# Delta-rule part of a two-layer decoder trunk on one core: TensorE's program order kept and rewritten, own products in one stretch each, inverse by levels

## The chip, the cores and the metric

The kernel runs on one core of one Trainium2 chip. The metric is the device time of one execution in microseconds (us). A core has five engines, each with an instruction stream of its own: TensorE (PE, matrix products into PSUM), VectorE (DVE), ScalarE (ACT), GpSimd (POOL) and SyncE (SP, here the issuer of most DMAs). They wait for each other through semaphores. Times of day below ("at 325.3") are microseconds from the start of the profiled span.

## The reference

`x` is 256 tokens of 1024 channels, float32. Two layers, each a half-step SwiGLU block, a mixer, and another half-step SwiGLU block, with an RMS norm ahead of each:

```
for l in range(DEPTH):                                   # DEPTH = 2
    h = h + 0.5 * swiglu(rms_norm(h, ffn1_norm[l]), ffn1_w_in[l], ffn1_w_out[l])
    u = rms_norm(h, mix_norm[l])
    (z_s, xbc, dt_s, qkv, z_d, b_d, a_d, gate_s, gate_d) = jnp.split(u @ w_in[l], split_points, axis=-1)
    y_s = mamba2_branch(...)                             # SSD, chunks of 128 tokens, 32 heads of 64
    y_d = deltanet_branch(...)                           # gated delta rule, chunks of 64 tokens, 8 heads of 128
    merged = sigmoid(gate_s) * (y_s @ ssm_w_branch[l]) + sigmoid(gate_d) * (y_d @ dn_w_branch[l])
    h = h + merged @ w_out[l]
    h = h + 0.5 * swiglu(rms_norm(h, ffn2_norm[l]), ffn2_w_in[l], ffn2_w_out[l])
return rms_norm(h, final_norm)
```

The change lies in the delta-rule branch. q, k and v pass a causal convolution of four taps and a SiLU. Then, for each head and chunk of 64 tokens:

```
M = where(strict, (kb @ k.T) * decay, 0)                 # kb = k * beta
sol = triangular_solve(eye + M, concat([v * beta, kb * exp(G)]))
u, w = sol[..., :dv], sol[..., dv:]
a_qk = (q @ k.T) * decay
# over the 4 chunks, one after the other:
v_new = u_c - w_c @ state
o = q_c @ state + a_c @ v_new
state = state * exp(gl) + k_c.T @ v_new
```

## The kernel before

**Products and weights.** Every float32 product is made of three products of reduced-precision parts: high·high, high·low, low·high. A weight tile (`wraw`, 128x1024, 512 KB) is fetched by SP into one of 5 buffers; ScalarE copies its high part (`whi`, in `act`, L68); VectorE subtracts to get the low part (`wlo`, in `tt`, L71); 5 pairs of `whi`/`wlo` can wait for TensorE. So each weight tile costs SP, ScalarE and VectorE one instruction each, in the order in which TensorE will use it.

**Bulk units.** The mixer's input projection is cut into units. A unit of channels (`kk`, `qq`, `vv` for k, q, v; `zd` the delta branch's gate; `bc` and `xs` of the SSD branch) takes two weight tiles and 48 products of 128x256 (`chan_chunk`; in the profile its three kinds of product are L340, L345 and L346). A unit of tokens (`t`, for z and the gates) takes two weight tiles and 24 products of 128x512 (L366). Behind each `kk`, `qq`, `vv`, `bc` and `xs` unit stands a convolution (`conv`): for each half an ACT instruction `ca`, three multiply-adds on VectorE (`stt`, L74) and an ACT SiLU that gives `kP`, `qP`, `vP`, a tile with the channels in partitions.

**The delta rule's small work.** Heads go in four pairs, `hp` 0 to 3.
- `turned` (L776): four TensorE transposes of `kP` or `qP` for the norms and for `kd`.
- `own` (L788): the products k·k (`kkb`) and q·k (`qkb`) of a chunk with itself, two heads beside each other. From `kkb` VectorE makes `Q`, the strict triangle M of each head and chunk (`tt`); from `qkb` it makes `AT`.
- `invert`: (I+M)⁻¹ for the 32 blocks of 64x64. The 16x16 diagonal blocks of `Q` go through DRAM (`dq1`, L866) into a layout `X` (L872), where VectorE sweeps over them (15 pairs of `tp` and `X`, then a COPY, L881), and come back (`dq2`, L882; then sixteen small DMAs into `T` and `TT`, L885 and L886). Then two doublings, to 32 and to 64: `yb` = Q·TT (L891), an eviction to `Y`, `wb` = T·Y, an eviction into `TT`. Before, each doubling is done for one half of the blocks after the other.
- `vtb` (L853): transposes of `vP`.
- `recur`: four chunks one after the other: `ksb`, `qsb` (k and q against the state, L954), `rh` on VectorE, `vnb` (L973), `sb` (the state's update, L981, with eight `stt` on VectorE), `ob` (L995).

After this part comes the SSD branch (`cbb`, L1045; `xsb`, L1101 on).

**The order.** The list `ORDER` names the steps in which the program is written: lower-case letters are units, K, Q and V the rest of a unit (turn, own products, norm), I a step of the inverse, R a step of the recurrence. A scheduler then lays out each engine's stream from its estimates and from priorities. The weight tiles follow the order of the units.

Of the kernel before, what the change touches and what calls it, by code (L numbers as in the profile page):

```python
# [16 lines left out]
P = 128  # L17
# [29 lines left out]
z20 s z10 z11 s z21 s M k1 k0 q1 k2 k3 K1 K0 q3 q0 K3 K2 v0 q2 I Q0 I Q3 I z30 v1 z31 Q2 v2 V0 I v3  # L47
V1 I V3 I Q1 V2 d0 R R R b3 R b2 b0 R b1 R d2 R x00 R d1 x01 R d3 R R P R g100 g101 D0 S0 x10 T0 D1
x11 g110 g111 S1 x20 T1 o x21 N D2 y S2 D3 x30 x31 T2 g000 g010 g001 S3 g011 T3
""".split()  # L50


@with_exitstack
def trunk_kernel(ctx, tc, x, wst, wsm, norms, lpar, rpar, cst, out):
    nc = tc.nc
    V, A, G, PE = nc.vector, nc.scalar, nc.gpsimd, nc.tensor
# [191 lines left out]
    for y in Y:  # L248
        G.memset(y[:], 0.0)
# [98 lines left out]
    def tok_chunk(ps, ks):  # L348

# [6 lines left out]
        for t, k0, (wh, wl) in order:  # L356
# [8 lines left out]
            for j, (st, mv) in enumerate(three):  # L365
# [8 lines left out]
                i += 1  # L374

    def chan_chunk(ps, cut=False):

        ws = [take(), take()]
        for a in range(2):
            for q in range(2):  # L380
                wh, wl = ws[q]
                for k in range(4):
                    kt = 4 * q + k
                    c0 = k * 256 + a * P
                    mm3w(
                        ps[:, a * 256 : (a + 1) * 256],
                        wh[:, c0 : c0 + P],
                        wl[:, c0 : c0 + P],
                        uTh[:, kt, :],
                        uTl[:, kt, :],  # L390
                        kt == 0,
                        kt == KT - 1,
                        cut and a == 0 and kt == 1,
                    )

# [197 lines left out]
    def mixer(l, nxt):  # L593
# [17 lines left out]
        def tok_unit(key, part, done):  # L611
# [3 lines left out]
            tok_chunk(open_[key], range(KT) if part is None else range(4 * part, 4 * part + 4))  # L615
# [4 lines left out]
        def z_unit(g, part):  # L620
            if part != 1:
                yz[g] = slots.tile([P, 2, 512], F32, tag=f"y{g}", name="yz")
            tok_unit(("z", g), part, lambda t, ps: act(yz[g][:, t, :], ps[:], AF.Silu))
# [13 lines left out]
        z_unit(0, None)  # L637
# [146 lines left out]
        def own(bank, x, y, hp):  # L784

            for c in range(4):
                for a in range(2):
                    PE.matmul(  # L788
                        bank[64 * a : 64 * a + 64, c * 64 : (c + 1) * 64], x[:, hp, c, a, :], y[:, hp, c, a, :],
                        start=True, stop=True,  # L790
                    )

        qev = {}

        def k_unit(hp):
            ps = accb("kk")
            chan_chunk(ps, hp == 1)
# [3 lines left out]
            def rest():  # L801
                ktb, nb = turned(kP, hp)
                ts(kq[:, hp], nb[:], EPS, ALU.add)
                c1 = small([P, 4], "c1")
                V.reciprocal(out=c1[:], in_=kq[:, hp])
                tt(c1[:], c1[:], Bp[:, hp], ALU.mult)
                stt(c3n[:, hp], c1[:], -1.0, eG[:, hp], ALU.mult, ALU.mult)
                kkb = trb("kkb")
                own(kkb, kP, kP, hp)
                kk = s2.tile([P, 4, 64], F32, tag="s2", name="kk")  # L810
                for c in range(4):
                    act(kk[:, c], kkb[:, c * 64 : (c + 1) * 64], scale=c1[:, c : c + 1])
                for a in range(2):
                    rows_ = slice(64 * a, 64 * a + 64)
                    qev["ins"] = tt(Q[rows_, 4 * hp : 4 * hp + 4, rows_], dN[rows_, 4 * hp : 4 * hp + 4], kk[rows_], ALU.mult)
                for c in range(3):
                    act(kd[:, c, hp, :], ktb[:, c * P : (c + 1) * P], scale=dT[:, 4 * hp + c, 63:64])
                rsqrt(c2[:, hp], kq[:, hp], [P, 4])
                G.tensor_tensor(out=c2[:, hp], in0=c2[:, hp], in1=Bp[:, hp], op=ALU.mult)
                yield  # L820

            return rest()

        def q_unit(hp):
            ps = accb("qq")
            chan_chunk(ps)
# [3 lines left out]
            def rest():  # L830
                _, nb = turned(qP, hp)
                ts(oe[:, hp], nb[:], EPS, ALU.add, EPS * 128.0, ALU.mult)
                qkb = trb("qkb")
                own(qkb, kP, qP, hp)
                for a in range(2):
                    rows_ = slice(64 * a, 64 * a + 64)
                    qk = qkb[rows_, 0:256].rearrange("p (c i) -> p c i", c=4)
                    tt(AT[rows_, 4 * hp : 4 * hp + 4, rows_], dT[rows_, 4 * hp : 4 * hp + 4], qk, ALU.mult)
                yield

            return rest()

        def v_unit(hp):
            ps = accb("vv")
            chan_chunk(ps, hp == 2)
            vP = s2.tile([P, 4, 2, 64], F32, tag="s2", name="vP")
# [3 lines left out]
            def rest():  # L850
                vtb = trb("vtb")
                for c in range(4):
                    PE.transpose(vtb[:, c * P : (c + 1) * P], vP[:, c].rearrange("p a i -> p (a i)"), ident)  # L853
                for c in range(4):
                    act(vb[:, c, hp, :], vtb[:, c * P : (c + 1) * P], scale=c2[:, hp, c : c + 1])
                yield

            return rest()

        def invert():  # L860
# [32 lines left out]
            for half in range(2):  # L893
                prs = list(range(8 * half, 8 * half + 8))
                p0 = prs[0]
                yb = trb("yb")
                for i, pr in enumerate(prs):
                    half_mm(
                        yb, i, Q[:, pr, :],
                        TT[:, pr, :].rearrange("p (b o s) -> p b o s", b=4, o=2)[:, :, 1, :],  # L900
                    )
                for w in range(2):
                    act(
                        Y[w][:].rearrange("p (x o s) -> p x o s", o=2, s=16)[:, :, 1, :],
                        yb[:, w * 256 : (w + 1) * 256].rearrange("p (x s) -> p x s", s=16),
                    )
                wb = trb("wb")
                for i, pr in enumerate(prs):
                    yv = Y[i // 4][:, (i % 4) * P : (i % 4 + 1) * P]
                    half_mm(wb, i, T[:, pr, :], yv.rearrange("p (b o s) -> p b o s", b=4, o=2)[:, :, 1, :])  # L910
                for b in range(4):
                    r0 = 32 * b
                    act(
                        TT[r0 : r0 + 16, p0 : p0 + 8, r0 + 16 : r0 + 32],
                        wb[r0 : r0 + 16].rearrange("p (x b s) -> p x b s", x=8, b=4)[:, :, b, :],
                        scale=-1.0,
                    )
                    if b % 2 == 0:
                        blk = (slice(r0, r0 + 32), slice(p0, p0 + 8), slice(r0, r0 + 32))
                        V.transpose(out=T[blk], in_=TT[blk])  # L920
                yield
            for half in range(2):
                prs = list(range(8 * half, 8 * half + 8))
                p0 = prs[0]
                Y2 = tmp2("Y2")
                yb = trb("yb2")
                for i, pr in enumerate(prs):
                    half_mm(yb, i, Q[:, pr, :], TT[:, pr, :].rearrange("p (b o s) -> p b o s", b=2, o=2)[:, :, 1, :])
                act(Y2[:], yb[:])
                wb = trb("wb2")  # L930
                for i, pr in enumerate(prs):
# [507 lines left out]
```

## Time and profile before

| | |
|---|---|
| median of 3 runs | 1543.06 us (1542.31 to 1544.37) |
| span of the profiled execution | 1539.7 us |
| first K product to first `xsb`, layer 0 | 228.03 to 415.28 |
| the same, layer 1 | 988.77 to 1176.64 |
| first `yb` of layer 0 | 325.32 |

The execution that was profiled is shown by its span, from the first to the last recorded instruction; the runs' times stand 3.4 us over it, with what lies around the span. A row of the order of time gives start, duration, engine, line, operation, tile written and tiles read, the shape, and how many instructions were merged into the row ("x4"); behind it, in brackets, idle time of the engine and what ended it. A matmul's duration includes its way through the array, so pitch is read from one start to the next.

### The profile page before, as it was taken

How to read it: one execution, taken by the hardware profiler on the slowest of the kernel's cores; microseconds unless marked ns; L12 is line 12 of the kernel's file. 1: busy time of each engine (PE TensorE's matmuls, PEld its weight loads, DVE VectorE, ACT ScalarE, POOL GpSimd, SP SyncE). 2: the span in 40 equal slices, each digit the busy share in tenths (PEclk: the TensorE clock that was granted, in tenths of full speed). 3: DMA queues.
4: the chain of work that ended last, by engine and by line, in shares of the span. 5: the costliest groups of instructions: out<-in, count | busy, mean ns of one | idle time of the engine just before them, and what ended most of it. 6: DMA issues, size and time to landing. Idle time of an engine off the chain costs nothing.

```text
span 1539.7 us, 29072 instructions
## 1 busy us (share of the span) xinstructions
PE 1522.8 (99%) x11473; PEld 1384.4 (90%) x11473; DVE 1229.7 (80%) x1859; ACT 944.8 (61%) x1532; POOL 81.8 (5%) x92
## 2 busy tenths in 40 slices
PE   8999999999999999999999999999999999999998
PEld 7999889999888888999899998899998888899997
DVE  6878769967899766789778887689589996677886
ACT  5655667765665645555555566676756666455565
POOL 0000110000000000000100012010000000000010
PEclk9999999999999999999999999999999999999999
DMA  7687775653565556587867687665345555556785
GB/s 277 190 265 231 226 228 167 187 164 111 178 213 171 163 166 196 185 256 211 261 225 225 208 253 229 197 193 180 117 141 202 179 170 186 176 177 195 247 241 156
DMA packets 98831, 305.73 MB, mean 199 GB/s; under 512 B 22837, under 2 KB 23813, under 8 KB 97670
## 3 DMA queue, kind: packets, MB, share of 16 engines
q1 hardware_dynamic: 93796, 290.95, 57.2%
q0 software_dynamic: 4608, 12.58, 5.1%
q8 instruction: 90, 1.47, 0.4%
q14 instruction: 47, 0.39, 0.1%
q10 hardware_dynamic: 290, 0.33, 0.1%
HBM read 297.72 MB, written 1.92 MB: 195 GB/s over the span
## 4 chain that ended last, share of the span: by engine, by line
PE 89%; DVE 4%; ACT 2%; DMA 2%; issue 1%; SPq 1%; POOL 0%; POOLq 0%; ACTq 0%; DVEq 0%
PE fc L346 10%; PE fc L340 9%; PE fc L345 9%; PE t L366 9%; PE o L337 4%; PE o L335 4%; PE o L336 4%; PE f L366 3%; PE b L335 3%; PE b L337 3%; PE b L336 3%; PE p L336 2%; PE p L337 2%; PE p L335 2%; PE xs L345 1%; PE xs L340 1%
## 5 line engine op out<-in xcount | busy, mean ns | idle before, releaser
L71 DVE TENSOR_TENSOR wlo<-wraw,whi 128x1024 fp32r<-128x1024 f32 x488 | 591.8, 1221 | 186.7 <-ACT whi L68 172.2
L68 ACT ACTIVATE whi<-wraw 128x1024 fp32r<-128x1024 f32 x488 | 511.6, 1059 | 271.0 <-PE fc L345 92.5
L346 PE MATMUL fc<-uW,wlo 128*128 128x256 f32 x1280 | 354.9, 277 | 0.0
L340 PE MATMUL fc<-uW,whi 128*128 128x256 f32 x1280 | 354.1, 277 | 0.0
L345 PE MATMUL fc<-uW,whi 128*128 128x256 f32 x1260 | 348.3, 276 | 0.0
L340 PEld LDWEIGHTS fc<-uW,whi 128*128 128x128 f32 x1280 | 240.5, 188 | 0.8
L346 PEld LDWEIGHTS fc<-uW,wlo 128*128 128x128 f32 x1280 | 240.5, 188 | 0.0
L345 PEld LDWEIGHTS fc<-uW,whi 128*128 128x128 f32 x1260 | 236.5, 188 | 0.8
L366 PE MATMUL t<-whi,uW 128*128 128x512 f32 x512 | 165.3, 397 | 0.0
L366 PEld LDWEIGHTS t<-whi,uW 128*128 128x128 f32 x512 | 95.9, 188 | 21.6 <-issue 1.3
L68 ACT ACTIVATE whi<-wsum 128x1024 fp32r<-128x1024 f32 x64 | 68.0, 1062 | 58.8 <-PE fc L345 32.9
L366 PE MATMUL t<-wlo,uW 128*128 128x512 f32 x256 | 100.2, 392 | 0.0
L71 DVE TENSOR_TENSOR wlo<-wsum,whi 128x1024 fp32r<-128x1024 f32 x64 | 78.2, 1221 | 7.9 <-ACT whi L68 5.6
L335 PE MATMUL b<-whi,bh 128*128 128x512 f32 x192 | 76.1, 398 | 0.3
L336 PE MATMUL b<-wlo,bh 128*128 128x512 f32 x192 | 74.9, 390 | 0.0
L337 PE MATMUL b<-whi,bl 128*128 128x512 f32 x192 | 74.2, 393 | 0.0
L340 PE MATMUL xs<-uW,whi 128*128 128x256 f32 x256 | 72.8, 284 | 0.0
L346 PE MATMUL xs<-uW,wlo 128*128 128x256 f32 x256 | 71.4, 279 | 0.0
L345 PE MATMUL xs<-uW,whi 128*128 128x256 f32 x254 | 70.6, 278 | 0.0
L335 PE MATMUL o<-whi,gh 128*128 128x512 f32 (+1 forms) x160 | 62.0, 388 | 0.0
L337 PE MATMUL o<-whi,gl 128*128 128x512 f32 (+1 forms) x160 | 61.8, 386 | 0.0
L336 PE MATMUL o<-wlo,gh 128*128 128x512 f32 (+1 forms) x160 | 61.7, 386 | 0.0
(337 smaller groups left out, 3291.7 us busy)
## 6 DMA issues: line engine op xcount, KB each, us to landing
wraw<-in_wst_dram SPq DMA_DIRECT2D x504, 512.0 KB, 4.9
wsum<-in_wst_dram SPq DMA_DIRECT2D x16, 512.0 KB, 7.3
wsum<-in_wst_dram POOLq DMA_DIRECT2D x16, 512.0 KB, 8.7
dc<-rdram SPq DMA_DIRECT2D x8, 1024.0 KB, 8.5
nw<-in_norms_dram SPq DMA_DIRECT2D x6, 512.0 KB, 5.9
h<-u POOLq DMA_DIRECT2D x12, 256.0 KB, 6.8
gb<-rdram SPq DMA_DIRECT2D x8, 256.0 KB, 5.6
h<-in_x_dram SPq DMA_DIRECT2D x4, 256.0 KB, 3.7
```

The costliest lines, as they stand in the source:

```text
L68: return A.activation(out=o, in_=i, func=func, **kw)
L71: return V.tensor_tensor(out=o, in0=a, in1=b, op=op)
L335: PE.matmul(ps, lh, rh, start=start, stop=False)
L336: PE.matmul(ps, lh, rl, start=False, stop=False)
L337: return PE.matmul(ps, ll, rh, start=False, stop=stop)
L340: PE.matmul(ps, wh, mh, start=start, stop=False)
L345: PE.matmul(ps, wh, ml, start=False, stop=False)
L346: PE.matmul(ps, wl, mh, start=False, stop=stop)
L366: ins = PE.matmul(ps[t][:], st, mv, start=k0 == 0 and j == 0, stop=k0 == KT - 2 and j == 5)
```

## The change

`ORDER` gets a new list for the delta rule. From the step `k1` to the step `g100` every TensorE instruction keeps the program's order (`Ordered`, `KEPT`): the scheduler no longer moves any of them against another. The generators (`yield`) let a unit be issued in pieces: `z31:6` is the first 6 steps of the unit, a later `z31` its rest. All TensorE rows of the changed kernel bear the lines of the wrapper (L63 product, L66 transpose).

```diff
-z20 s z10 z11 s z21 s M k1 k0 q1 k2 k3 K1 K0 q3 q0 K3 K2 v0 q2 I Q0 I Q3 I z30 v1 z31 Q2 v2 V0 I v3
-V1 I V3 I Q1 V2 d0 R R R b3 R b2 b0 R b1 R d2 R x00 R d1 x01 R d3 R R P R g100 g101 D0 S0 x10 T0 D1
-x11 g110 g111 S1 x20 T1 o x21 N D2 y S2 D3 x30 x31 T2 g000 g010 g001 S3 g011 T3
+z20 s z10 z11 s z21 s M k1 k0 q1 k2 k3 q3 KO K10 q2 K32 I q0 I v0 QO Q32 v1 V0 Q01 v2 V1 v3 V2 z30 I
+z31:6 I z31 I V3 I b3:8 R b3 R d0:8 R d0 b2:4 R b2 R d1 R b0 R b1:10 R b1 d2:10 R d2 x00:10 R x00 x01:4 R x01 d3 R
+P g100 g101 D0 S0 x10 T0 D1 x11 g110 g111 S1 x20 T1 o x21 N D2 y S2 D3 x30 x31 T2 g000 g010 g001 S3 g011 T3
 """.split()
+KEPT = ("k1", "g100")
...
+        def put(self, ins):
+            if self.kept:
+                tc.keep_in_program_order(ins)
+            return ins
...
-    for y in Y:
-        G.memset(y[:], 0.0)
...
+        def own(pairs, x, y, name):
+            banks = {}
+            for hps in pairs:
+                bank = trb(name)
+                for i, hp in enumerate(hps):
+                    banks[hp] = bank[:, 256 * i : 256 * i + 256]
+                    for c in range(4):
+                        for a in range(2):
+                            PE.matmul(
+                                banks[hp][64 * a : 64 * a + 64, c * 64 : (c + 1) * 64],
+                                x[:, hp, c, a, :], y[:, hp, c, a, :], start=True, stop=True,
+                            )
+            return banks
...
+        def own_k():
+            kkbs.update(own(((1, 0), (3, 2)), kP, kP, "kkb"))
+
+        def own_q():
+            for hp, qkb in own(((0, 1), (2, 3)), kP, qP, "qkb").items():
                 for a in range(2):
                     rows_ = slice(64 * a, 64 * a + 64)
+                    qk = qkb[rows_].rearrange("p (c i) -> p c i", c=4)
                     tt(AT[rows_, 4 * hp : 4 * hp + 4, rows_], dT[rows_, 4 * hp : 4 * hp + 4], qk, ALU.mult)
...
+            for n in (4, 2):
+                w = 64 // n
+                order = (0, 1) if n == 4 else (1, 0)
+                ys = [trb("yb") for _ in range(2)]
+                ev = Y if n == 4 else [tmp2("Y2") for _ in range(2)]
+                for half in order:
+                    for i in range(8):
+                        half_mm(ys[half], i, Q[:, 8 * half + i, :], odd(TT[:, 8 * half + i, :], n))
+                    act(ev[half][:], ys[half][:])
                 yield
+                ws = [trb("wb") for _ in range(2)]
+                for half in order:
+                    for i in range(8):
+                        half_mm(ws[half], i, T[:, 8 * half + i, :], ev[half][:, i * 64 : (i + 1) * 64])
...
         for name in ORDER:
+            if name in KEPT:
+                PE.kept = not PE.kept
             step(name)
```

`KO` issues the own K products of all four pairs, two pairs to a PSUM bank, `QO` the own Q products; K10, K32, Q32, Q01 are the turns and the rest of these pairs.

**TensorE at the own K products.** Before, at the end of the last K unit, the first two pairs are turned and multiplied one after the other:

```order
L340 MATMUL kk<-uW,whi 128x256
L345 MATMUL kk<-uW,whi 128x256
L346 MATMUL kk<-uW,wlo 128x256
L776 MATMUL turned<-cs,kP 128x128 x4
L788 MATMUL kkb<-kP 64x64 x8
L776 MATMUL turned<-cs,kP 128x128 x4
L788 MATMUL kkb<-kP 64x64 x8
```

After, one Q unit (q3) stands behind the last K unit, and then all four pairs' products:

```order
L63 MATMUL qq<-uW,whi 128x256 x2
L63 MATMUL qq<-uW,wlo 128x256
L63 MATMUL kkb<-kP 64x64 x32
L66 MATMUL turned<-cs,kP 128x128 x8
L63 MATMUL qq<-uW,whi 128x256 x2
```

The products of pairs 3 and 2 have moved ahead by two Q units, and their turns stand a unit (q2) behind them.

**TensorE at the own Q products.** Before, they stood in three places, two pairs behind the third Q unit and one pair each between steps of the inverse. After, they stand together, one V unit behind the last Q unit:

```order
L63 MATMUL vv<-uW,whi 128x256 x2
L63 MATMUL vv<-uW,wlo 128x256
L63 MATMUL qkb<-qP,kP 64x64 x32
L66 MATMUL turned<-cs,qP 128x128 x8
L63 MATMUL vv<-uW,whi 128x256 x2
```

All 32 now wait for the convolved tiles of the last Q unit. VectorE, there, before:

```order
L71 TENSOR_TENSOR AT<-dT,qkb 64x4x64 x3
L74 SCALAR_TENSOR_TENSOR ca<-qq,lp,ca 128x255
L71 TENSOR_TENSOR wlo<-wraw,whi 128x1024
L74 SCALAR_TENSOR_TENSOR ca<-qq,lp,ca 128x254
L71 TENSOR_TENSOR wlo<-wraw,whi 128x1024
L74 SCALAR_TENSOR_TENSOR ca<-qq,lp,ca 128x253
L79 TENSOR_SCALAR oe<-nb 128x4
L71 TENSOR_TENSOR tp<-X,X_3388 128x15
```

and after:

```order
L91 SCALAR_TENSOR_TENSOR ca<-qq,lp,ca 128x253
L91 SCALAR_TENSOR_TENSOR ca<-vv,lp,ca 128x253
L91 SCALAR_TENSOR_TENSOR ca<-vv,lp,ca 128x255
L91 SCALAR_TENSOR_TENSOR ca<-vv,lp,ca 128x254
L88 TENSOR_TENSOR AT<-dT,qkb 64x4x64
L91 SCALAR_TENSOR_TENSOR ca<-vv,lp,ca 128x253
L88 TENSOR_TENSOR AT<-dT,qkb 64x4x64 x6
L88 TENSOR_TENSOR tp<-X,X_3237 128x15
L88 TENSOR_TENSOR AT<-dT,qkb 64x4x64
```

Seven of the eight `AT` products of the chunk now stand ahead of the first step of the sweep, `tp`.

**TensorE at the first step of the inverse.** Before, `yb` of one half comes behind a stretch of `bc`:

```order
L340 MATMUL bc<-uW,whi 128x256
L345 MATMUL bc<-uW,whi 128x256
L346 MATMUL bc<-uW,wlo 128x256
L891 MATMUL yb<-TT,Q 64x64 x16
L340 MATMUL bc<-uW,whi 128x256
L345 MATMUL bc<-uW,whi 128x256
```

After, `yb` of both halves comes behind 24 products of a `t` unit:

```order
L63 MATMUL t_3779<-wlo,uW 128x512
L63 MATMUL t_3779<-whi,uW 128x512
L63 MATMUL yb<-TT,Q 64x64 x32
L63 MATMUL t_3778<-whi,uW 128x512
L63 MATMUL t_3778<-wlo,uW 128x512
```

Ahead of `yb` stood 48 `zd`, 66 `bc` and 48 `t` products beside K, Q and V before; now 24 `t` products do. The rest is behind it, between the steps of the inverse and of the recurrence.

More of the change, by code (lines that the diff above doesn't have):

```diff
@@ L348, in tok_chunk, with tok_steps @@
     def tok_chunk(ps, ks):
+        for _ in tok_steps(ps, ks):
+            pass
+    def tok_steps(ps, ks):
         ws = [(k, take()) for k in ks[::2]]
@@ new lines, in q_unit, with q_rest @@
+        def q_unit(hp):
+            ps = accb("qq")
+            yield from chan_steps(ps)
+            for a in range(2):
+                conv(ps[:, a * S : (a + 1) * S], 8 + 2 * hp + a, qP[:, hp, :, a, :], False)
+        def q_rest(hp):
+            _, nb = turned(qP, hp)
+            ts(oe[:, hp], nb[:], EPS, ALU.add, EPS * 128.0, ALU.mult)
+        def own_k():
+            kkbs.update(own(((1, 0), (3, 2)), kP, kP, "kkb"))
+        def own_q():
+            for hp, qkb in own(((0, 1), (2, 3)), kP, qP, "qkb").items():
@@ L820, in rest @@
[L820 to L826, printed above, removed]
-            for a in range(2):
-                conv(ps[:, a * S : (a + 1) * S], 8 + 2 * hp + a, qP[:, hp, :, a, :], False)
[L830 to L837, printed above, removed]
+                    qk = qkb[rows_].rearrange("p (c i) -> p c i", c=4)
@@ L1021, in bc_unit @@
             ps = accb("bc")
[L1022 removed]
+            yield from chan_steps(ps)
             for a in range(2):
```

192 lines of the change are left out of this document (81 added, 111 removed).

## The prediction

> **What bounds the kernel now.** I read the page first (span, engines, the chain that ended last), then TensorE's waits, then busy time by stretch, then single rows of the order of time.
>
> ```profile
> span 1539.7 us, 29072 instructions
> PE 1522.8 (99%) x11473; PEld 1384.4 (90%) x11473; DVE 1229.7 (80%) x1859; ACT 944.8 (61%) x1532; POOL 81.8 (5%) x92
> PE 89%; DVE 4%; ACT 2%; DMA 2%; issue 1%; SPq 1%; POOL 0%; POOLq 0%; ACTq 0%; DVEq 0%
> ```
>
> TensorE is busy 99% of the span and carries 89% of the chain. The three runs have a median of 1543.06, 3.4 over this span; I make the sum on the span and carry the 3.4 along. Waits of TensorE from the first K product of layer 0 to the first `xsb`, and its largest one behind that point in the whole program:
>
> ```profile
> PE cbb L1045 <- DVE vb L71: 0.6, 1, 0.6
> PE wb L891 <- ACT Y L68: 0.5, 2, 0.3
> PE xsb L1101 <- ACT xsT L68: 1.9, 2, 0.9
> ```
>
> So TensorE hardly ever waits now. What it leaves is a question of cover: how far behind are the engines that feed it? Busy time by stretch (K, K own products, Q own products, up to the first `yb`, from there to `xsb`, and the end of the kernel):
>
> ```profile
> core 0: us, PE busy (x) PEld busy (x) DVE busy (x) ACT busy (x) POOL busy (x), PEclk, DMA share, GB/s
> 228.00:256.00 28.00, 28.00 (x249) 27.83 (x248) 24.91 (x52) 21.03 (x35) 0.00 (x0) 1.00 0.56 185
> 256.00:269.40 13.40, 13.40 (x139) 12.93 (x140) 10.92 (x28) 11.15 (x43) 3.33 (x4) 1.00 0.50 155
> 269.40:283.40 14.00, 14.00 (x153) 13.46 (x154) 12.52 (x29) 12.28 (x43) 2.41 (x4) 1.00 0.51 154
> 283.40:325.30 41.90, 41.90 (x327) 39.55 (x327) 35.82 (x79) 22.78 (x46) 0.00 (x0) 1.00 0.60 173
> 325.30:415.30 90.00, 88.90 (x952) 81.87 (x952) 67.21 (x122) 60.52 (x135) 4.03 (x4) 1.00 0.48 155
> 1533.50:1539.70 6.20, 0.00 (x0) 0.00 (x0) 1.49 (x4) 1.23 (x3) 0.55 (x1) 0.68 0.22 85
> ```
>
> VectorE is busy 24.91 of 28.00 and 12.52 of 14.00 us (89%) while K and Q run, 75% behind `yb`. It is the engine with no slack in just the stretch that is rewritten. The points of time that the sum uses, on TensorE:
>
> ```profile
> 228.03 0.36 PE L340 MATMUL kk<-uW,whi 128*128 128x256 f32 x1
> 255.10 0.28 PE L340 MATMUL kk<-uW,whi 128*128 128x256 f32 x1
> 255.44 0.60 PE L776 MATMUL turned<-cs,kP 128*128 128x128 f32 x4
> 282.15 0.60 PE L776 MATMUL turned<-cs,qP 128*128 128x128 f32 x4
> 282.68 0.69 PE L788 MATMUL qkb<-qP,kP 128*64 128x64 f32 x16
> 283.29 0.66 PE L776 MATMUL turned<-cs,qP 128*128 128x128 f32 x4
> 325.12 0.28 PE L346 MATMUL bc<-uW,wlo 128*128 128x256 f32 x1
> 325.32 1.15 PE L891 MATMUL yb<-TT,Q 128*64 128x64 f32 x32
> 326.40 0.38 PE L340 MATMUL bc<-uW,whi 128*128 128x256 f32 x1
> 326.63 0.28 PE L345 MATMUL bc<-uW,whi 128*128 128x256 f32 x1
> 414.81 0.39 PE L366 MATMUL t<-wlo,uW 128*128 128x512 f32 x1
> 415.04 0.40 PE L366 MATMUL t<-whi,uW 128*128 128x512 f32 x1
> 415.28 0.27 PE L1101 MATMUL xsb<-cs,xsT 128*128 128x128 f32 x1
> ```
>
> Three products from 255.10 to 255.44: 0.113 us for one of 256 columns, 5.45 for a unit of 48. One of 512 columns takes 0.23 (414.81 to 415.04), so 24 take about 5.45 too. `kk` to `xsb` is 187.25 us (228.03 to 415.28). The last K product ends at 255.44, the last Q product of the third Q unit at 282.15. When their convolved tiles came (ScalarE), the pitch of VectorE, and the chain to the inverse (VectorE and SP):
>
> ```profile
> 236.45 1.22 DVE L71 TENSOR_TENSOR wlo<-wraw,whi 128x1024 fp32r<-128x1024 f32 x1
> 263.83 0.42 ACT L68 ACTIVATE kP<-ca 128x256 f32<-128x256 f32 x1
> 294.93 0.42 ACT L68 ACTIVATE qP<-ca 128x256 f32<-128x256 f32 x1 [0.15 <-DVE oe L79]
> 246.37 2.35 DVE L71 TENSOR_TENSOR wlo<-wraw,whi 128x1024 fp32r<-128x1024 f32 x2
> 248.64 0.47 DVE L74 SCALAR_TENSOR_TENSOR ca<-kk,lp,ca 128x255 f32<-128x255 f32 x1
> 249.03 0.47 DVE L74 SCALAR_TENSOR_TENSOR ca<-qq,lp,ca 128x255 f32<-128x255 f32 x1
> 280.99 0.87 DVE L71 TENSOR_TENSOR Q<-dN,kk 64x256 f32<-64x256 f32 x2 [0.85 <-ACT kk L68]
> 294.83 0.17 DVE L71 TENSOR_TENSOR tp<-X,X 128x15 f32<-128x15 f32 x1
> 309.90 0.39 DVE L881 COPY X<-X 128x256 f32<-128x256 f32 x1
> 310.31 0.33 SPq L882 DMA_DIRECT2D dq<-X  x1
> 314.54 0.33 SPq L885 DMA_DIRECT2D T<-dq  x1
> 322.92 0.45 SPq L886 DMA_DIRECT2D TT<-dq  x1
> ```
>
> From the end of the last K product to `kP` ready: 264.25 − 255.44 = 8.8 us. From the end of a Q unit to its `qP`: 295.35 − 282.15 = 13.2. From the end of the COPY (310.29) to `yb` (325.32): 15.0, of which 8.8 are SP issuing sixteen small DMAs.
>
> **The change part by part** (layer 0's mixer; layer 1 has the same order).
>
> *Removed.* The products are the same. Between `kk` and `xsb` the orders hold 1054 products of 256 columns and 96 of 512 on both sides; the number of times that TensorE changes to another kind of work falls from 81 to 62. A change costs about 0.1 us: `yb` starts 0.20 behind the product before it instead of 0.11, and the first `bc` behind it takes 0.23. So 19 × 0.1 = 2 us, with the 1.1 of recorded waits 3. Going through the whole order with the row's pitch for each kind gives about 180 where before measured 187.25; so 3 is the low and 7 the high end of what can be gained per mixer. I take 7 for an order without any wait, and add the waits below. The four memsets of `Y` and four ScalarE evictions cost nothing now (POOL 5%, ScalarE 61% busy) and bring nothing.
>
> *KO: own K products in one stretch.* Before, each head pair had its own stretch, and the late pairs came two Q units later. Now all four stand one Q unit (5.45) behind the last K unit. TensorE is there at 255.44 + 5.45 = 260.9; the first bank (pairs 1, 0) takes 1.2 (0.62 per 16), and at 262.1 the second needs pair 3's `kP`, ready at 264.25 by the row. Stall 2.1; I take 2.6, since VectorE's order has the q3 unit's convolution among K's there. Ends: 0 (if VectorE puts nothing between) and 4.
>
> *QO: own Q products in one stretch.* It follows the last Q unit, q0, after only one V unit (5.45), and its first bank is pair 0 and 1. Behind KO stand a bank, 16 turned products in two places and three units: TensorE is there at 264.7 + 1.2 + 2.1 + 16.3 = 284.1, and q0 ended at 278.6. With K's lag of 8.8, `qP` is ready at 287.4, with Q's of 13.2 at 291.8. A second way: VectorE's own work. From 236.45 (its first `wlo` in this stretch) the new order gives it, up to q0's last convolution step, 19 subtractions at 1.13 (the pair in the row takes 2.35, and the next instruction starts 0.08 before its end), 50 convolution steps at 0.39 (248.64 to 249.03), 8 `Q` products at 0.44 and some 3.5 of small ones: 49 us, so 286 with no wait at all. Taking the waits for the own products' evictions into account I get 290.9, close to the Q row, because the same `Q` products stand in between. Stall 6.8; ends 2.5 and 7.7. KO and QO together set TensorE 9.4 back; that alone is more than the 7 gained.
>
> *The chain to `yb`.* Pair 2's and 3's `Q` now hang on KO's second bank and the turned K tiles behind it; I get the last at 283.3 against 281.86. The diagonal blocks reach VectorE at about 294, as before. But the first step of the sweep (`tp`, 294.83 before) now stands behind seven `AT` products, which wait for QO: 295.7. Of the 30 steps' company, four of six weight subtractions are gone (−4.5) and one `AT` and an `oe` have come: COPY ends at 308 instead of 310.29, and with the row's 15.0 `yb` can start at 323; earliest 319.4 (no wait on VectorE), latest 325. SP, past which this moves, has loaded the weights of everything up to some 20 us behind `yb` by then, so the sixteen DMAs in front of the next weights starve nobody. TensorE gets there at about 319 to 321 and waits 2 to 4.
>
> *Behind `yb`.* Here lies the price. Before, the chain was covered by 48 `zd`, 66 `bc` and 48 `t` products. Now only 24 `t` products of these stand ahead of `yb`: 114 × 0.113 + 24 × 0.227 = 18.4 us move behind it. Ahead of it come instead two pairs' turned and own Q products and three V turns, 4.1. From `yb` to `xsb` was 89.96; now 89.96 + 18.4 − 4.1 = 104.3, less 4 of the gain above (most broken stretches lay here): 100. So `xsb` at 323 + 100 = 423 against 415.3, **+8 per mixer**.
>
> *Levels and recurrence.* Each pass of the inverse now covers its eviction and VectorE's transpose by 12 `t` products (2.7 us) or the other half; each recurrence step by 24 to 48 products (2.7 to 5.5). The longest link, the state's update (eight steps at 0.39 and a conversion, some 4.3), has a 6.5 us cover. I cost these at nothing; if VectorE is late there by one 1.13 subtraction, that is 1 us per place. The `cbb` wait goes.
>
> *After `xsb`.* The order is the same. VectorE and ScalarE, no longer chased, may lose the 0.9 of `xsb`'s wait: −1 per mixer.
>
> Sum: 2 × (8 − 1) = 14, on the span 1553.7, on the runs **1557**. Layer 1's own length is the same within 0.7:
>
> ```profile
> 988.77 0.37 PE L340 MATMUL kk<-uW,whi 128*128 128x256 f32 x1
> 1176.64 0.49 PE L1101 MATMUL xsb<-cs,xsT 128*128 128x128 f32 x3
> ```
>
> **The rivals.**
>
> *Feeders in time (faster).* If convolutions are done when the own products come, KO and QO do not wait and `yb` follows at 309: up to −7 per mixer, 1529. It decides at `qP` before 282 and the COPY before 294. Against it: 49 us of VectorE work from 236.45. In part it can hold: with stalls of 6 in all and `yb` no bar, 1538 to 1541. Chance 0.13.
>
> *Break-even.* QO ready at 286.5 and the chain at its earliest, 319.4: `xsb` at 419.4, less 1, would be +3 per mixer, 1549; it takes another 3 of gain behind `yb` to be within 0.2% (3.1 us, about what a measurement here tells from no change). Chance 0.09 for within.
>
> *The clock.* In the last 6.2 us no product runs and the mean clock is 0.68: full for 2.2 us, then half, if half is what it drops to. A stall of 6.8 (QO) would then drop it, those at KO and `yb` (2.6, 2 to 4) may. What a restart costs stands nowhere clean here: the first ten products of the kernel (four turns and six of 512 columns, 0.5 + 1.4 by the pitches above) took 3.3, so 1.4 bounds it loosely.
>
> ```profile
> 9.90:13.20 3.30, 3.30 (x10) 2.46 (x11) 3.30 (x5) 2.72 (x5) 0.00 (x0) 1.00 1.02 417
> ```
>
> With 1 us for each of three stalls, QO's hidden in `yb`'s wait, it is +2 to +3 per mixer: 1562. Chance 0.17. The Trainium skill ("TensorE: Matmul & The Clock Gate", Part 1) has a gap of about 3.4 us as the point where the clock halves and about 3.4 us of work to get it back; by that only QO's stall would count, for an estimated 1.7 us, inside `yb`'s wait, and the sum would stay. The 2.2 of the row speaks for an earlier drop than the page's.
>
> *Kept order without slip.* With TensorE pinned, one late operand stops everything behind it, where before the scheduler's order had room. If two or three recurrence links each miss their cover by one subtraction, +2 to +4 per mixer, 1564. Chance 0.11.
>
> My forecast itself (1546 to 1560) has 0.50; faster 0.13, same 0.09, slower 0.78. The range reaches from 1541 (half of the gain without stalls) to 1568 (clock and recurrence together).
>
> **What would show it.** Right: TensorE's waits name `kkb` for ScalarE's `kP` (about 2.6 each), `qkb` for `qP` (about 6.8) and `yb` for the `TT` DMAs (2 to 4), twice each; `yb` at 323 and `xsb` at 423 if `kk` still starts at 228; TensorE idle about 25 us more in all, and busy some 10 less. Wrong: no wait at `qkb`, `yb` before 316, or `yb` to `xsb` under 95. Wrong most easily by the place of `qP` on VectorE, which is counted and not seen.

## The result, and the profile after

The changed kernel takes 1567.56 us (median of 4 runs, 1562.60 to 1568.81) against 1543.70 of the kernel before (4 runs, 1542.31 to 1544.37): 24 us more, a ratio of 1.0147 with an interval of [1.0130, 1.0164]. It is slower, as forecast, by more than the forecast's 14: above the 1546 to 1560 that the forecast itself was given, and just under the 1568 at which its range ended. The profiled execution has a span of 1567.0, and its time, 1568.81, stands 1.8 above that, so it lies at the upper end of the runs. Its span is 27.3 above that of before, where the medians are 24 apart: with the same 1.8, not the 3.4 taken above, the profiled execution of before took about 1541.5, a little less than its runs.

The page's first lines and TensorE's waits over the whole program (engine, tile, line, then the engine and tile waited for; us in all, how often, longest):

```profile
span 1567.0 us, 29056 instructions
PE 1528.4 (98%) x11473; PEld 1393.0 (89%) x11473; DVE 1232.2 (79%) x1859; ACT 947.6 (60%) x1528; POOL 77.1 (5%) x90
PE 87%; DVE 6%; ACT 4%; issue 2%; DMA 1%; SPq 0%; POOL 0%; POOLq 0%; ACTq 0%; DVEq 0%
PE qkb L63 <- ACT qP L85: 14.1, 4, 4.7
PE kkb L63 <- ACT kP L85: 5.2, 2, 2.8
PE b L63 <- ACT bh L85: 2.7, 2, 1.4
PE hnT L66 <- DVE hn L91: 2.4, 2, 1.3
PE yT L66 <- DVE og L91: 2.4, 2, 1.2
```

Of these only `hnT` stood on the list before. `kkb` is new, once per mixer, and `qkb`, twice per mixer, and so are `b` and `yT`, which stand behind the rewritten part. Layer 0's mixer in the order of time (TensorE, then the ScalarE, VectorE and SP rows that its waits name):

```profile
228.88 0.36 PE L63 MATMUL kk<-uW,whi 128*128 128x256 f32 x1
265.88 1.15 PE L63 MATMUL kkb<-kP 128*64 128x64 f32 x30 [2.79 <-ACT kP L85]
290.16 0.47 PE L63 MATMUL qkb<-qP,kP 128*64 128x64 f32 x2 [4.65 <-ACT qP L85]
293.11 3.68 PE L63 MATMUL qkb<-qP,kP 128*64 128x64 f32 x62 [2.48 <-ACT qP L85]
324.21 2.08 PE L63 MATMUL yb<-TT,Q 128*64 128x64 f32 x64
425.49 0.38 PE L66 MATMUL xsb<-cs,xsT 128*128 128x128 f32 x2
292.64 0.42 ACT L85 ACTIVATE qP<-ca 128x256 f32<-128x256 f32 x1 [1.80 <-DVE ca L91]
298.55 0.16 DVE L88 TENSOR_TENSOR tp<-X,X 128x15 f32<-128x15 f32 x1
311.15 0.38 DVE L908 COPY X<-X 128x256 f32<-128x256 f32 x1
321.69 0.45 SPq L913 DMA_DIRECT2D TT<-dq  x1
```

The profile has two rows for each of these small products, 64 for a stretch of 32. TensorE stands 2.8 us in the middle of the own K products and 7.1 us at the own Q products: it runs two rows, one product, when the first half of `qP` is there, and the other 62 rows when the second half is (292.64 + 0.42). `kk` to `xsb` is 196.6 us against 187.25. The last term lies behind that point. `mT` is the first work behind both branches; rows of before, then of after:

```profile
568.98 0.28 PE L1264 MATMUL mT<-cs,tg 128*128 128x128 f32 x1
457.31 0.74 DVE L74 SCALAR_TENSOR_TENSOR og<-oT,lp,zdT 128x512 f32<-128x512 f32 x1
```

```profile
582.99 0.28 PE L66 MATMUL mT<-cs,tg 128*128 128x128 f32 x1
467.63 1.47 PE L66 MATMUL oT<-cs,vb 128*128 128x128 f32 x12
469.50 0.75 DVE L91 SCALAR_TENSOR_TENSOR og<-oT,lp,zdT 128x512 f32<-128x512 f32 x1
470.30 0.66 PE L66 MATMUL yT<-cs,yz 128*128 128x128 f32 x4 [1.20 <-DVE og L91]
470.40 1.33 ACT L85 ACTIVATE yz<-yz,srr 128x512 f32<-128x512 f32 x2 [0.25 <-POOL srr L227]
472.31 0.80 PE L63 MATMUL b<-whi,bh 128*128 128x512 f32 x1 [1.35 <-ACT bh L85]
```

`xsb` to `mT` was 153.7 (415.28 to 568.98) and is 157.5: 3.8 us more per mixer in a part whose list of steps did not change. Measured from `xsb`, `og` comes 2 us later than before (44.0 behind it against 42.0). `bh`, made of `og` on ScalarE, comes later still, at 471.64, since ScalarE takes `yz` first. In layer 0 that makes 9.35 + 3.8 = 13.15; in layer 1 (`kk` 1002.82, `xsb` 1200.03, `mT` 1357.57; before 988.77, 1176.64, 1330.25) 9.34 + 3.9. The two are 26.4 of the 27.3, and the rest (0.9) came in the first block ahead of the first `kk`, which the change does not touch.

The clock, by stretch of the changed kernel (columns as before; PEclk is the third from the end):

```profile
285.40:288.00 2.60, 0.11 (x1) 0.00 (x0) 2.57 (x6) 1.97 (x3) 0.00 (x0) 0.99 0.86 218
288.00:293.10 5.10, 0.47 (x2) 0.29 (x2) 4.88 (x9) 1.57 (x5) 0.00 (x0) 0.50 0.80 199
293.10:298.30 5.20, 5.19 (x71) 5.07 (x71) 3.96 (x10) 1.61 (x7) 0.00 (x0) 0.51 0.41 149
470.00:472.30 2.30, 0.66 (x4) 0.42 (x4) 1.78 (x4) 2.00 (x4) 0.36 (x1) 1.00 0.75 212
472.30:476.00 3.70, 3.69 (x9) 3.01 (x10) 3.70 (x7) 1.39 (x3) 0.00 (x0) 0.54 0.42 152
```

It halves 2.4 us after the last product ahead of QO and stays so through the 5.2 us of work behind the wait, and it is half again in the first 3.4 us of `b`.

### The profile page after: what moved, and what is told of

It is laid out like the page before. It is cut to its first block, busy times and chain, and to the rows that moved or that the text cites. A ratio compares the mean times of both kernels' runs of the same rounds, so it can differ in the third digit from the quotient of the medians.

```text
span 1567.0 us, 29056 instructions
## 1 busy us (share of the span) xinstructions
PE 1528.4 (98%) x11473; PEld 1393.0 (89%) x11473; DVE 1232.2 (79%) x1859; ACT 947.6 (60%) x1528; POOL 77.1 (5%) x90
## 4 chain that ended last, share of the span: by engine, by line
PE 87%; DVE 6%; ACT 4%; issue 2%; DMA 1%; SPq 0%; POOL 0%; POOLq 0%; ACTq 0%; DVEq 0%
PE fc L63 28%; PE o L63 11%; PE t L63 11%; PE b L63 8%; PE p L63 6%; PE xs L63 5%; PE f L63 3%; PE zd L63 3%; PE bc L63 3%; DVE wlo L88 2%; DVE ca L91 2%; PE ydb L63 1%; ACT whi L85 1%; ACT x L85 1%; PE kk L63 1%
## 5 line engine op out<-in xcount | busy, mean ns | idle before, releaser
L63 PE MATMUL fc<-uW,whi 128*128 128x256 f32 x2580 | 440.4, 276 | 0.0
L63 PEld LDWEIGHTS fc<-uW,whi 128*128 128x128 f32 x2580 | 389.9, 188 | 1.6
L63 PE MATMUL fc<-uW,wlo 128*128 128x256 f32 x1280 | 354.9, 277 | 0.0
L63 PEld LDWEIGHTS fc<-uW,wlo 128*128 128x128 f32 x1280 | 240.6, 188 | 0.0
L63 PE MATMUL t<-whi,uW 128*128 128x512 f32 x512 | 165.4, 397 | 0.0
L63 PEld LDWEIGHTS t<-whi,uW 128*128 128x128 f32 x512 | 95.9, 188 | 21.3 <-issue 0.8
L63 PE MATMUL t<-wlo,uW 128*128 128x512 f32 x256 | 100.0, 392 | 0.0
L63 PE MATMUL xs<-uW,whi 128*128 128x256 f32 x514 | 92.4, 283 | 0.0
L63 PE MATMUL b<-whi,bh 128*128 128x512 f32 x192 | 77.4, 405 | 2.7 <-ACT bh L85 2.7
L63 PEld LDWEIGHTS xs<-uW,whi 128*128 128x128 f32 x514 | 78.7, 189 | 1.0 <-issue 1.0
L63 PE MATMUL b<-wlo,bh 128*128 128x512 f32 x192 | 76.3, 397 | 0.0
L63 PE MATMUL b<-whi,bl 128*128 128x512 f32 x192 | 75.7, 396 | 0.0
L63 PE MATMUL xs<-uW,wlo 128*128 128x256 f32 x256 | 71.5, 279 | 0.0
L63 PE MATMUL o<-whi,gh 128*128 128x512 f32 (+1 forms) x160 | 62.0, 387 | 0.0
L63 PE MATMUL o<-whi,gl 128*128 128x512 f32 (+1 forms) x160 | 61.7, 386 | 0.0
L63 PE MATMUL o<-wlo,gh 128*128 128x512 f32 (+1 forms) x160 | 61.7, 386 | 0.0
L63 PEld LDWEIGHTS t<-wlo,uW 128*128 128x128 f32 x256 | 48.1, 188 | 10.5 <-DVE ca L91 0.5
L63 PEld LDWEIGHTS xs<-uW,wlo 128*128 128x128 f32 x256 | 48.2, 188 | 0.0
```

The source lines that it names most:

```text
L63: return self.put(nc.tensor.matmul(*args, **kw))
```

## The experiments

The diffs are pieces of `ORDER`; "..." stands for what is left out. Their "-" lines are the changed kernel's, in 9 and 10 run 8's.

**1. TensorE not pinned.** Everything as changed, but the scheduler may move TensorE's instructions.

```diff
-KEPT = ("k1", "g100")
+KEPT = ()
```

> The rewritten list, own products and levels as in the changed kernel, but TensorE's order left to the scheduler. It then puts 23 V products ahead of half of the own Q products and 48 t, 55 bc and 48 zd products ahead of yb; behind xsb its order is that of the changed kernel (oT x12, yT x4, b x96). Theory (the pinned QO and the thin cover ahead of yb cost some 9 us up to xsb in each mixer, the order behind xsb another 4): the 9 go for the most part, the 4 stay, so 1548 to 1554. Rival (pinning costs nothing, the rewritten list makes ScalarE and VectorE late whatever TensorE does): 1562 to 1568, with a qkb wait near 7 us.

Measured: 1550.74 us, ratio 1.0036 [1.0021, 1.0052], as its theory had it. TensorE's waits of layer 0 up to `xsb`, the largest three:

```profile
PE kkb L63 <- ACT kP L85: 1.7, 1, 1.7
PE qkb L63 <- ACT qP L85: 1.0, 1, 1.0
PE yb L63 <- ACT TT L85: 0.7, 1, 0.7
```

`kk` to `xsb` is 188.65 in layer 0, 1.4 above the kernel before (9.35 with pinning), and in layer 1 it is the same as before; `xsb` to `mT` is 3.1 and 2.7 above it, with TensorE's order there as in the changed kernel. So 8 to 9 us per mixer come from the rewritten list with TensorE held to it, and some 3 from something behind it.

**2. The own Q products one V unit later; 3. and a `zd` unit ahead of `yb`.** Both pinned.

```diff
...
-K32 I q0 I v0 QO Q32 v1 V0 Q01 v2 V1 v3 V2 z30 I
+K32 I q0 I v0 v1 QO Q32 V0 v2 Q01 V1 v3 V2 z30 I          # 2
+K32 I q0 I v0 v1 QO Q32 V0 v2 Q01 V1 v3 V2 d0 z30 I       # 3 (the later units moved up)
...
```

> QO one V unit (5.45 us) later, all else pinned as in the changed kernel. Theory: the qkb wait falls from 7.1 to under 2 us in each mixer and the clock stays full (granted clock 1.00 from 284 to 304, where it was down to 0.50); the sweep no longer stands behind the AT products, so COPY ends some 4 us earlier, but yb now waits for TT: only about 4 us per mixer come back, 1559 to 1561. Rival (the QO stall alone sets yb, the TT chain has slack): all 7.3 per mixer come back, 1552 to 1554.

> As the run with QO one V unit later, and a zd unit (48 products, 5.45 us) moved ahead of yb, the recurrence covered by the remaining nine units. Theory: TensorE reaches yb when TT has landed, no wait there, no new wait in the recurrence: 7 us per mixer come back, 1551 to 1555. Rival (the recurrence needs the unit that was taken): waits at vnb, ksb or ob, and no better than the run with QO alone moved, 1558 to 1562.

Measured: 2 gave 1572.69, ratio 1.0175 [1.0156, 1.0193], worse than the change itself; 3 gave 1561.84, 1.0108 [1.0090, 1.0125]. Both theories for 2 were wrong. Its waits in layer 0, and the clock around KO:

```profile
PE yb L63 <- DMA TT<-dq: 3.9, 1, 3.9
PE vtb L66 <- DVE AT L88: 3.3, 1, 3.3
PE kkb L63 <- ACT kP L85: 3.0, 1, 3.0
PE qkb L63 <- ACT qP L85: 1.1, 1, 1.1
262.00:276.00 14.00, 10.98 (x127) 10.77 (x127) 10.02 (x25) 10.89 (x41) 2.43 (x4) 0.88 0.44 144
```

The `qkb` wait went from 7.1 to 1.1, as meant, and 3.3 came back at the first V turn, which wants a PSUM bank that `AT` still reads, and 3.9 at `yb`, since the sweep began no earlier (298.77) and its COPY came 2 us later (313.21). In addition the 3.0 at KO now cost the clock (0.88 over 14 us is half for 3.4), where the 2.8 in layer 0 of the changed kernel had not, and the clock was half for 3.4 us again at the V turn and at `yb`. Run 3 puts bulk into the `yb` wait, which goes, and keeps the rest; it ends in its rival's range, but no wait of the recurrence stands in its profile. In these two runs a wait that VectorE causes was not removed by moving the waiter; it went to the next one.

**4. Pinning the last part of the delta branch too; 5. its first transposes one step earlier.** The 3.8 us behind `xsb`.

```diff
-KEPT = ("k1", "g100")
+KEPT = ("k1", "g100", "N", "S2")                          # 4
...
-x20 T1 o x21 N D2 y S2
+x20 o T1 x21 N D2 y S2                                    # 5
...
```

> The changed kernel, and TensorE's program order kept in the delta branch's last part too, so that oT and b alternate and yT comes behind b. Theory (the 3.8 us per mixer behind xsb come from the scheduler's hoisting of yT ahead of b): the waits at yT and b (2.4 and 2.7 us in all) go, 1559 to 1562. Rival (VectorE and ScalarE are late there in any order): 1566 to 1569, with the waits at oT and b in their place.

> The changed kernel with the step o (the first four oT transposes of the delta branch's last part, their og, bh and bl) written one step earlier, ahead of T1 instead of behind it; TensorE's order up to xsb is untouched, behind it oT x4 now stands ahead of ydb and 18 b products ahead of the next oT and of yT. Theory (the 3.8 us per mixer behind xsb come from og of the first pair being late on VectorE, after which TensorE idles 1.2 and 1.4 us and then runs b at half clock): og is made ahead of need, the yT and b waits go, 1559 to 1562. Rival (VectorE is behind there altogether and what is moved ahead delays ydb's operands instead): 1566 to 1570.

Measured: 4 gave 1576.26, ratio 1.0201 [1.0185, 1.0217], slower than its theory and its rival; 5 gave 1560.77, 1.0112 [1.0099, 1.0125], 7 us below the change, as its theory had it. In 4 `oT` and `b` alternate, and `b` waits 4.1 for `bh`:

```profile
472.39 0.50 PE L63 MATMUL b<-whi,bh 128*128 128x512 f32 x1 [4.07 <-ACT bh L85]
```

In 5 VectorE makes `og` at 462.26, 7 us earlier, the wait at `yT` is gone, the clock stays full there, and `xsb` to `mT` is 154.3, 0.6 above the kernel before:

```profile
462.26 0.74 DVE L91 SCALAR_TENSOR_TENSOR og<-oT,lp,zdT 128x512 f32<-128x512 f32 x1
579.23 0.28 PE L66 MATMUL mT<-cs,tg 128*128 128x128 f32 x1
460.00:468.00 8.00, 8.00 (x91) 7.45 (x88) 8.00 (x15) 3.11 (x6) 0.00 (x0) 1.00 0.61 207
```

So the place of `yT` was not the cause; `og` late on VectorE was (in the kernel before it stood at 457.31, ahead of the last twelve `oT`). Why the scheduler put it later there is not shown.

**6. The inverse by levels alone,** put into the kernel before with its own list.

> The kernel before, with the inverse by levels alone (both halves' yb, both evictions, both wb; no cleared Y); the list of steps and TensorE's freedom are those of before, and behind xsb the order is the same. Theory (the inverse by levels is neither the loss nor worth more than its two or three fewer changes of work): 1541.5 to 1545. Rival (a part of the loss is the levels': TensorE has to wait for both halves' evictions): 1546 to 1552, with waits at wb and yb of 1 us or more each.

Measured: 1543.63, ratio 0.9999 [0.9990, 1.0008]. It waits 1.2 us at `yb` and 0.5 at `wb` per mixer, which may be what its fewer changes of work save. In the order of before, then, the levels cost nothing.

**7. Not pinned, KO one Q unit later, `o` earlier; 8. pinned, everything later and more cover, `o` earlier.** In 8, 48 `zd` and 48 `t` products stand ahead of `yb`.

```diff
...
-q3 KO K10 q2 K32 I q0 I v0 QO Q32 v1 V0 Q01 v2 V1 v3 V2 z30 I
+q3 q2 KO K10 q0 K32 I v0 I QO Q32 v1 V0 Q01 v2 V1 v3 V2 z30 I       # 7
+q3 q2 KO K10 q0 K32 I v0 I v1 QO v2 Q32 V0 v3 Q01 V1 V2 d0 z30 z31 I  # 8
...
```

Not shown: in 7 `KEPT` is empty; in both `o` stands a step earlier, as in run 5, and so it does in 9 to 12; in 8 the units behind `yb` are spread anew between the steps of the inverse and of the recurrence.

> TensorE's order left to the scheduler as in the run without pinning, KO one Q unit later (behind q2), step o written one step earlier. Theory (what is left of that run's loss is the kkb wait, 2.7 in all, and the part behind xsb, 3 us per mixer): 1542 to 1546. Rival (a later KO puts the chain to yb behind its cover): a yb wait of 2 us or more in each mixer, 1548 to 1552.

> Pinned as in the changed kernel, but with more room: KO one Q unit later, QO two V units behind the last Q unit and a third V unit between QO and the turns, 48 zd and 48 t products ahead of yb, 24 bc products between the passes of the inverse, and step o one step earlier. Theory (a kept order is no loss where each own product and yb has its 10 to 13 us or more of cover): no wait over 1 us at kkb, qkb or yb, granted clock 1.00, 1540 to 1546. Rival (VectorE's own load is the limit in this stretch, so the waits reappear at the V turns behind the AT products, as they did when QO alone was moved): 1550 to 1560.

Measured: 7 gave 1549.33, ratio 1.0042 [1.0028, 1.0056], 3 us over the top of its theory. The time is its rival's, but the wait is not: in layer 0 it has 2.5 us at a V turn and 2.3 at turned tiles, and 0.2 at `yb`. 8 gave 1547.27, 1.0031 [1.0019, 1.0043], between theory and rival: `kkb`, `qkb` and `yb` wait for nothing, but a V turn wants a bank that ScalarE has not yet read, and the clock drops there:

```profile
306.83 0.90 PE L66 MATMUL vtb<-cs,vP 128*128 128x128 f32 x3 [3.90 <-ACT x L85]
300.00:326.00 26.00, 21.52 (x124) 19.25 (x123) 18.95 (x58) 17.12 (x58) 0.00 (x0) 0.87 0.44 121
```

**9. and 10. The same with that clump spread** (V0 to V2 and Q01 each 24 to 48 products apart; in 10 Q01 behind the first `wb`).

```diff
...
-v1 QO v2 Q32 V0 v3 Q01 V1 V2 d0 z30 z31 I b3:8 I b3 I
+v1 QO v2 Q32 v3 V0 d0 V1 z30 Q01 z31 V2 I b3:8 I b3 I          # 9
+v1 QO v2 Q32 v3 V0 d0 V1 z30 V2 z31 I b3:8 I Q01 b3 I          # 10
...
```

> The pinned order with more cover, and the turned Q tiles of two pairs and the V turns no longer back to back: each now stands 24 to 48 products from the next (V0 behind the fourth V unit, V1 behind zd, Q01 and V2 between and behind the halves of the two t units). Theory (what was left there was one clump: ScalarE's reads of the turned tiles hold the PSUM banks that the V turns want, 3.9 us, and the clock then drops, 2 us): both go, so some 6 us per mixer less than the run with the clump, 1533 to 1538, below the kernel before. Rival (VectorE is the limit in the stretch, so the wait reappears at the next thing that needs it, vtb for vP or yb for TT): 1543 to 1549.

> As the run with the spread order, but the turned Q tiles of the pairs 0 and 1 behind the first wb, so that ScalarE has eight reads fewer ahead of yb. Theory (ScalarE's queue between 296 and 312 is what holds the V turns): as good or up to 2 us better, 1532 to 1538. Rival (the eight reads then stand in front of TT's eviction, and yb of the second pass waits): 1 to 3 us worse per mixer than the other run of this call.

Measured: 1564.61, ratio 1.0134 [1.0119, 1.0149], and 1565.86, 1.0137 [1.0120, 1.0154]. The rival of 9 was right in where the wait reappears, at `yb` for `TT`, but the time is 16 us beyond its range. 10 is 1.25 us above 9, which their runs do not tell apart, with the same wait (14.1). In 9, TensorE is at `yb` at 322.4; the sweep ended less than 2 us before, and its way back through DRAM takes 15.5:

```profile
302.49 0.17 DVE L88 TENSOR_TENSOR tp<-X,X 128x15 f32<-128x15 f32 x1
320.31 0.39 DVE L908 COPY X<-X 128x256 f32<-128x256 f32 x1
336.25 0.44 PE L63 MATMUL yb<-TT,Q 128*64 128x64 f32 x3 [13.84 <-DMA TT<-dq]
```

From its first step to the COPY the sweep took 12.6 us in the changed kernel and takes 17.8 here: six weight subtractions and 16 convolution steps come between its steps, against two and six there. It also begins later, since KO late means `Q` late; but run 8 has KO in the same place, begins the sweep at 300.33, has its COPY at 314.09 and does not wait at `yb`. Of the 8.3 us by which `yb` starts later than there, 2.2 are the later start of the sweep, 4.1 its length and 2.1 the way back; and TensorE is at `yb` 5.5 us earlier than there (327.92).

**11. and 12. The chain started early.** The own K products in two places again, as in the kernel before (`KA` for pairs 1 and 0, `KB` for 3 and 2), QO three units behind the last Q unit, the sweep's step (the second I) ahead of it, and 144 products of bulk ahead of `yb`, against 162 in the kernel before; 11 pinned, 12 not.

```diff
...
-k3 q3 KO K10 q2 K32 I q0 I v0 QO Q32 v1 V0 Q01 v2 V1 v3 V2 z30 I z31:6 I z31 I V3 I
+k3 KA K10 q3 q0 KB K32 I v0 q2 I z30 v1 z31 QO v2 Q32 v3 V0 d0 Q01 V1 b3 V2 I b2:8 I b2 I V3 I
...
```

Not shown: the units behind this piece are spread anew between the steps of the recurrence, and in 12 `KEPT` is empty.

> Pinned, but with the own K products in the two places where the kernel before had them (two pairs behind the last K unit, two behind the next two Q units), QO behind a V and a t unit, no V turn next to a turned Q tile, 48 t, 48 zd and 48 bc products ahead of yb, and 24 products or more between the recurrence's steps; VectorE's order then has the sweep ahead of most AT products. Theory (the loss is the late start of the chain from the own K products to TT, and own products too close behind their convolutions; with both undone a kept order can use its fewer changes of work): waits at kkb, qkb and yb under 2 us each, 1536 to 1541, at or below the kernel before. Rival (VectorE cannot do the sweep, the V convolutions and the weights in time, so yb waits again): a yb wait of 4 us or more per mixer, 1547 to 1555.

> The same list with TensorE's order left to the scheduler, which here changes two places only (10 more bc products ahead of yb, two inside the second wb). Theory (with a list that has room, pinning or not makes no difference): within 2 us of the pinned run, 1536 to 1542. Rival (the pinning itself costs, by TensorE's strict order): 3 us or more below the pinned run.

Measured: 1539.97, ratio 0.9974 [0.9965, 0.9983], and 1539.62, 0.9975 [0.9965, 0.9986]. Both beat both kernels, by 4 us and by 28, as their theories had it, and pinning makes no difference between them that the runs can tell. No wait at `kkb`, `qkb` or `yb` is left in the pinned one; the largest it has in this part is a V unit that wants its accumulator from a convolution of VectorE, and the clock drops there:

```profile
PE vv L63 <- DVE ca L91: 3.8, 2, 1.9
292.00:298.00 6.00, 6.00 (x41) 6.00 (x41) 3.44 (x9) 1.82 (x3) 0.00 (x0) 0.72 0.88 319
```

Whether a list without that wait would gain another few us was not tried. Nor do these two runs tell apart what they change together: the place of KO, the place of QO, the cover ahead of `yb` and the earlier `o`.

## Why the prediction was right, point by point

- **KO.** The stall was to be 2.6; it is 2.8 and 2.4 in the two mixers.
- **QO.** 6.8 forecast, 7.1 and 7.0 measured. VectorE's own load and the lag of 13.2 us from a Q unit to its `qP` gave it: q0's last product starts at 279.80 here and the second half of `qP` is ready at 293.06, 13.3 later. Three slips of the working do not move the result: the Q unit that ended at 282.15 was the last of four, not the third; TensorE's arrival adds up to 284.3, not 284.1; and VectorE's own work to 48 us, not 49.
- **The chain to `yb`.** 323 forecast, 324.21 measured, of which 0.85 is the later start; that it came so near is partly luck. Two terms were off and cancelled: with the later start taken off, the sweep began 2 us later than I had it (QO went on 1.4 later than 290.9, and the first `AT` product waited 0.6 for own products that ran at half clock), while COPY to `yb` took 12.7 instead of 15.0. TensorE was to wait 2 to 4 there for the `TT` DMAs and waited for nothing: it came that much later itself, with QO's delay and the clock's loss.
- **What fewer changes of work save.** The prediction took 7 per mixer, the high end of its 3 to 7; the runs show less. From `kk` to `xsb` of layer 0, in the kernel before, in run 1 and in the changed kernel, the first figure behind the comma is TensorE's busy time:

```profile
228.03:415.28 187.25, 186.15 (x1813) 175.59 (x1813) 151.34 (x307) 127.70 (x299) 9.77 (x12) 1.00 0.52 163
228.27:416.92 188.65, 183.78 (x1813) 174.97 (x1812) 150.33 (x307) 131.28 (x298) 9.64 (x12) 1.00 0.52 160
228.88:425.49 196.61, 185.95 (x1813) 177.49 (x1812) 155.64 (x309) 131.63 (x298) 9.66 (x12) 0.97 0.50 156
```

Run 1, at full clock, takes 2.4 us less. The changed kernel takes 3.0 less by an estimate that counts half of its 5.6 us of work at half clock in this stretch as lost, and 3.5 in layer 1 (186.90, with 8.6 at half clock, against 186.13). With the 1.1 of waits that is 3.5 to 4.6, not 7, and the half clock hides it: TensorE is busy 5.6 us more in the whole program (1528.4 against 1522.8), where the prediction had some 10 less.
- **Behind `yb`.** 100 forecast, 101.3 measured. Levels and recurrence cost nothing, as said; the profile lists no wait of TensorE at `wb`, `vnb`, `ksb`, `sb` or `ob`.
- Up to `xsb`, then, +9.35 against +8. The stalls at KO and QO were right; the rest of the agreement is luck, since a saving taken too high, a wait at `yb` that did not come and a loss of clock that the sum put at nothing cancelled.
- **After `xsb`: the step that failed.** "The order is the same" was wrong, and −1 was +3.8 per mixer: 4.8 of the 6 us by which the sum per mixer missed. The list's tail is the same, but the scheduler laid it out otherwise: `og` moved behind other work on VectorE, two idle spells of 1.2 and 1.4 us followed (the second with ScalarE taking `yz` ahead of `bh`), and the first 3.4 us of `b` ran at half clock. Run 1 has the same two spells with the clock full and loses 3.1 and 2.7, so the idle time is the larger part. Run 5, with one step moved, took 3.2 per mixer of it back by its profile, and 6.8 in the median.
- **The rivals.** The clock rival was half right: stalls did halve it, in layer 0 at QO and at `b`, in layer 1 at KO too, and nowhere at `yb`. With QO at half clock the 62 rows, the turned tiles behind them and the rest up to 298.3 lose half of 5.2 us, 2.6, more than the 1.4 that bounded a restart. TensorE is busy at half clock for 9.0 us in layer 0 and 12.0 in layer 1; half of that, 4.5 and 6.0, is an estimate of what the clock cost per mixer, and the sum had it at nothing. "Kept order without slip" was wrong for the recurrence, and run 12 against 11 shows that pinning costs nothing where the list has room. In the changed kernel it cost 8 to 9 us per mixer, since the scheduler otherwise repairs the list (run 1). "Feeders in time" was wrong: `qP` came at 293, not before 282, and the COPY at 311, not before 294; with the waiters moved later (runs 2, 3 and 8) waits came back further on.

## What to carry to other kernels

Before work is drawn together into one stretch, count the lag from the last input of the stretch to its operand on the engines between (here 9 to 13 us through ScalarE and VectorE) and put at least that much other work between; then ask which long chain starts from the stretch's results, since what covers that chain has to stand ahead of its end. A list that pins an engine gives up the scheduler's repair and gains nothing by itself. And compare the orders of all engines outside the rewritten part as well: a changed list upstream moved an instruction on VectorE behind it, and that was over a quarter of the loss (6.8 of 24 us, run 5).

## What the runs showed of the hardware that I had not expected

The clock halves sooner and for longer than I had priced, and no length of wait decides it. It dropped 2.4 us after the last product at QO; it dropped at `b` after idle spells of only 1.2 and 1.4 us with four transposes between them; a wait of 3.0 us at KO dropped it in run 2, 1.5 us after the wait was over. Of the changed kernel's two waits at KO the 2.8 of layer 0 did not drop it, and the 2.4 of layer 1 did. It came back after 3.4 us of work at `b` and 5.1 at QO.

It follows a grid in time instead. In the changed kernel's record of the granted clock the half-clock stretches begin at 287.97, 472.29, 1038.90, 1062.79 and 1247.11, whole multiples of 3.413 us apart, and each lasts one or three times 3.413. Here are windows of that grid: KO of layer 0, the one ahead of the drop at QO, the three at half clock and the next; then KO of layer 1 and the one behind it.

```profile
264.07:267.49 3.42, 1.61 (x35) 1.54 (x36) 3.38 (x6) 1.23 (x3) 0.00 (x0) 1.00 0.75 214
284.56:287.97 3.41, 0.95 (x9) 0.76 (x7) 3.18 (x8) 2.81 (x3) 0.00 (x0) 1.00 0.73 174
287.97:298.21 10.24, 5.57 (x71) 5.27 (x72) 8.78 (x18) 3.09 (x10) 0.00 (x0) 0.50 0.61 175
298.21:301.62 3.41, 3.41 (x31) 3.41 (x30) 2.51 (x13) 1.84 (x15) 0.00 (x0) 1.00 0.00 0
1035.49:1038.90 3.41, 1.55 (x38) 1.28 (x36) 3.38 (x6) 2.96 (x5) 0.00 (x0) 1.00 0.58 172
1038.90:1042.31 3.41, 2.86 (x35) 2.75 (x36) 2.38 (x4) 0.42 (x1) 0.00 (x0) 0.50 0.77 249
```

TensorE's busy time within a window (the first figure behind the comma) tells the two apart: behind 1.61 us the clock stayed full, behind 1.55 and 0.95 it was half. In the 14 traces of this case, each on its own grid, all windows at full clock with 1.54 us of busy time or less (34) were followed by half clock and none with 1.59 or more, with two and two between; at half clock all with 2.79 or less stayed there (29), and all with 2.86 or more went back to full (34). So a wait of 2.4 to 3 us costs clock or not by where it falls on the grid. Where the grid lies differs between executions (the recorded clock becomes full at 13.33 in the trace of before and at 14.90 in the changed kernel's), and this may be why the changed kernel's four runs spread by 6 us: the fastest has a mean granted clock of 0.994, the slowest 0.989.

The Trainium skill ("TensorE: Matmul & The Clock Gate", Part 1) has a free-running window of about 3.4 us and a restart that varies with where in the window the work begins; the traces agree, with 3.413. The gap of about 3.4 us that the prediction took from the Trainium skill is not needed here: a window with 1.55 us of work in it was enough, and the measurement decides.
